# TensorE in the order of the source: grouped side work of the mixer and means of split operands in a two-layer decoder step

## Chip, cores and metric

The kernel runs on one core of a Trainium2 chip. The time is device time in microseconds (us) for one execution, which computes the whole decoder step. PE is TensorE (matmuls), DVE is VectorE, ACT is ScalarE, POOL is GpSimd, SP is SyncE, which only issues DMAs here.

## What is computed

A two-layer decoder trunk of width 1024 takes 256 prompt tokens and 8 sample sequences of 8 tokens. All 320 token columns go through the same weights in one pass.

```python
x += 1/2 * SwiGLU_1(RMSNorm(x))
h  = RMSNorm(x);  [u | v | q | g] = h @ W_in
A  = pool_mixer(u)            # trailing windows 2/4/8/16, a 256x256 map for each of 4 groups
B  = conv(v)                  # GLU, causal depthwise conv of width 31, LayerNorm, swish, W_pw
C  = cross_attend(q, k, v)    # 4 heads of 256 over 256 memory tokens
x += (sig(gA)*A + sig(gB)*B + sig(gC)*C) @ W_out
x += 1/2 * SwiGLU_2(RMSNorm(x))
```

For the prompt, memory keys and values come out of a projection of memory tokens; for the samples they are read from caches, and the pooling and the conv continue from stored rows. All numbers are float32.

## The kernel before

Activations lie feature-major: 8 tiles of 128 features by 320 tokens. Weights stream from HBM in the order of use; a unit is 8 blocks of 128x128. A product is exact to about float32 because weight and activation are each split in two fp32r halves (`whi`, `wlo`; `hhi`, `hlo`), and `chain` (L299) issues three matmuls for each block: hi*hi, hi*lo for the blocks of a unit, then lo*hi for them (L306, L307, L309). Eight blocks make a chain of 24 matmuls for one 128-feature output. `whi` is a cast on ACT, `wlo` a subtraction on DVE, or, for half of the units inside the mixer, a copy and an accumulating DMA on POOL's queue (L225 to L227). Splits run three units ahead of PE (`LA`).

Side work is a generator that `pump` (L276) steps once for each unit: the norm, the conv, pooling, softmax. `defer` (L257) puts a piece off by so many units. The program text thus gives every engine an order, but in the kernel before it is not the order that runs: the tile framework's scheduler, which simulates a timeline, may move instructions on every engine, PE too, as long as operands and buffers allow it. Engines then run their queues in order.

In the mixer of a layer (L683) PE projects memory keys and values, then v, q, and for each of four groups g two u chains, the two pool maps of the group before (short chains of two blocks), and two gate chains; then gates for branch C with the attention values, gates for branch B, W_pw and W_out. Small products lie between the chains:

- `prompt_scores` (L620 the scores of a head, L630 the four transposes of its softmax),
- `sample_scores` (L640: 8 matmuls for a batch, each 32 rows wide, in four column groups of the array), the transposes of its softmax (L652),
- the attention values of a block (L837) and of the samples (`sample_values`, L665), and the transposes of those (L677),
- means over features: a matmul with a constant matrix of 1/1024 in plain float32 (`mean_bc`, L354; the first one in eight pieces, L901). The prompt's norms, the memory and the conv's LayerNorm use them.

PSUM has eight banks: three under the tag `mm` for chains, two each under `cv` and `st`, one under `sa`. In a group the two u chains, two pool maps and two gate chains go through the three `mm` banks in turn, so the second pool map needs the bank of the first u chain, which ACT's copy to `ut` (L773) gives back, and the first gate chain needs that of the second u chain.

The depthwise conv of the prompt runs as two lanes of 31 multiply-adds on DVE in the `cv` banks (`conv_lane`), that of the samples on POOL (`conv_sample`), block after block; ACT moves each block's sample result to its place (L538), after DVE has ended the same block. Then the eight blocks are summed for the mean.

Of the kernel before, what the change touches and what calls it, by code (L numbers as in the profile page):

```python
# [7 lines left out]
F32 = mybir.dt.float32  # L8
# [7 lines left out]
P = 128  # L16
# [19 lines left out]
RC = 3.0  # L36
RN = 6.0
# [47 lines left out]
def trunk_kernel(  # L85
# [16 lines left out]
    nc = tc.nc  # L102
    const = ctx.enter_context(tc.tile_pool(name="const", bufs=1))
# [55 lines left out]
    ones = const.tile([P, P], F32, name="ones")  # L159
    pool.memset(ones[:, :], 1.0 / 1024.0)  # L160
# [191 lines left out]
    def mean_bc(acc, n, tag="st"):  # L352
# [21 lines left out]
    def ffn(h, mean, on_block, at_down=None):  # L374
# [8 lines left out]
        def stat():  # L383
            rsqrt_now(mean(), T, rstd[:, :])

        defer(stat, 2)
        for j in range(NJ):
            pg = pwide()
            chain(pg[:, :T], xs, T)
            sg = t320("sg")  # L390
# [6 lines left out]
            if j == 0:  # L397
                chain(pu[:, :T], xs, T)
                ev_gate()
            else:  # L400
                ev_gate()
                chain(pu[:, :T], xs, T)
            up = t320("up")
            dve.tensor_tensor(out=up[:, :], in0=pu[:, :T], in1=rstd[:, :], op=ALU.mult)
            dve.tensor_tensor(out=up[:, :], in0=up[:, :], in1=sg[:, :], op=ALU.mult)

            def fin(j=j, up=up):
                split_plain(up[:, :], *ref(j))

            defer(fin)  # L410
# [24 lines left out]
    def mem_operands(l, box):  # L435
# [20 lines left out]
        if l == 0:  # L456
            m = mean_bc(acc[:, :NM], NM)
            yield
            rsqrt_now(m, NM, rmem[:, :])
# [81 lines left out]
    def conv_gen(l, z, zdone, ch, gate):  # L541
# [32 lines left out]
        var = mean_bc(work[0], T, "cv")  # L574
# [96 lines left out]
    def sample_out(po, ats, g):  # L671
        ex = tp.tile([P, 2, NM], F32, name=nm("exo"), tag="ex", bufs=2)
        nc.scalar.copy(ex[:, 0, :], po[:, :256])
        yield
# [8 lines left out]
    def mixer(l, mh, acc, on_block):  # L683
        hn = []

        def norm_gen():
            rsqrt_now(mean_bc(acc[:, :], T), T, rstd[:, :])
# [13 lines left out]
        defer(lambda: start("norm", norm_gen(), 4), 2)  # L701
# [62 lines left out]

        for g in range(4):
# [3 lines left out]
            start("att", prompt_scores(q, g), 1)  # L769
# [57 lines left out]
        for o in range(KB):  # L827
            pc = pmm()
            chain(pc[:, :T], xs, T)
            s = t320("sgc")  # L830
            nc.scalar.activation(s[:, :TP], pc[:, :TP], AF.Sigmoid)
            nc.scalar.activation(sgs[:, o, :], pc[:, TP:T], AF.Sigmoid)
            hd, e = divmod(o, 2)
            pv = pst()
            clk["pe"] += 0.86
            for mb in range(2):
                nc.tensor.matmul(pv[:, :TP], vt[:, mb, o * P:o * P + P], kt[:, 2 * hd + mb, :],  # L837
                                 start=(mb == 0), stop=(mb == 1))

            def ev(o=o, s=s, pv=pv):  # L840
                dve.tensor_tensor(out=s[:, :TP], in0=pv[:, :TP], in1=s[:, :TP], op=ALU.mult)
                dve.tensor_tensor(out=merged[:, o, :TP], in0=merged[:, o, :TP], in1=s[:, :TP], op=ALU.add)

            defer(ev)
            if o == 0:
                drain("ss")
            if o == 1:
                pool_maps(3)
            if o % 4 == 0:
                drain("so")  # L850
                po = psum("sa", 1)
            if o % 2 == 1:
                sample_values(l, pps[o // 4], po, o - 1)
                sample_values(l, pps[o // 4], po, o)
# [41 lines left out]
    def first_mean():  # L896
        m = pst()
        for o in range(KB):
            s = t320("sq")
            pool.tensor_tensor(out=s[:, :], in0=x[:, o, :], in1=x[:, o, :], op=ALU.mult)  # L900
            nc.tensor.matmul(m[:, :T], ones[:, :], s[:, :], start=(o == 0), stop=(o == KB - 1))  # L901
# [160 lines left out]
```

## Time and profile before

| | us |
|---|---|
| median of 3 runs | 1659.54 |
| lowest, highest | 1659.35, 1659.97 |
| the profiled execution | 1659.87 |
| its span (mean granted TensorE clock 0.997) | 1657.9 |
| PE busy | 1630.5 (98%) |
| DVE busy | 1120.4 (68%) |
| ACT busy | 784.0 (47%) |
| POOL busy | 266.7 (16%) |

Matmuls overlap: one that streams 320 columns is shown with some 310 ns, while the next starts 147 ns after it. The spacing of starts is what counts, and busy shares say little about PE. A plain float32 matmul appears as two records. Lines in the trace are those of the kernel before.

### The profile page before, as it was taken

To read this page: it belongs to the slowest core of one execution; us is meant where nothing else is said; L and a number is where in the kernel's file an instruction comes from. 1 tells how busy PE (TensorE), PEld (TensorE's weight loads), DVE (VectorE), ACT (ScalarE), POOL (GpSimd) and SP (SyncE) were. 2 spreads that over 40 slices of the span, in tenths; PEclk is the share of its full clock that TensorE was granted. 3 is DMA by queue.
4 is the path that set the end of the run, shared out by engine and by line. 5 is a ranking of instruction groups with operands and counts; after the bars stand their busy time and mean duration, and the time that the engine had idled before them with its cause. 6 is when DMAs were issued, how large, how long until landed. Compare 5 with 4: busy or idle time off the path is not lost.

```text
span 1657.9 us, 27271 instructions
## 1 busy us (share of the span) xinstructions
PE 1630.5 (98%) x11194; PEld 1585.8 (96%) x11194; DVE 1120.4 (68%) x1854; ACT 784.0 (47%) x1167; POOL 266.7 (16%) x292
## 2 busy tenths in 40 slices
PE   8999999999999999999999999999999999999996
PEld 7999999998889999999999999999988899999996
DVE  7555647999975675554565564579998757655543
ACT  5444534456665444443344443354566544444341
POOL 2000001677520000000000000046674000000000
PEclk9999999999999999999999999999999999999998
DMA  7444446978976444444444444577798754444430
GB/s 276 153 151 145 169 169 199 266 231 238 294 260 229 151 155 151 144 146 149 149 153 153 153 153 166 189 220 232 235 278 254 267 199 153 145 145 147 150 126 32
DMA packets 47325, 305.73 MB, mean 184 GB/s; under 512 B 5728, under 2 KB 5792, under 8 KB 14048
## 3 DMA queue, kind: packets, MB, share of 16 engines
q1 hardware_dynamic: 38160, 270.75, 45.4%
q0 software_dynamic: 8752, 32.90, 9.2%
q8 instruction: 88, 1.44, 0.3%
q10 hardware_dynamic: 288, 0.33, 0.1%
q14 instruction: 37, 0.30, 0.0%
HBM read 295.14 MB, written 8.82 MB: 183 GB/s over the span
## 4 chain that ended last, share of the span: by engine, by line
PE 86%; DVE 7%; issue 3%; DMA 3%; ACT 1%; POOL 0%; DVEq 0%; SPq 0%; ACTq 0%; POOLq 0%
PE mm L306 19%; PE mm L309 19%; PE mm L307 19%; PE cv L309 8%; PE cv L306 8%; PE cv L307 8%; DVE cv L124 3%; DMA raw<-in_kc 2%; DVE us L124 1%; DVE wlo L124 1%; PE sa L665 1%; PE mm L484 1%; PE mm L483 1%; PE mm L487 1%; PE st L837 1%
## 5 line engine op out<-in xcount | busy, mean ns | idle before, releaser
L124 DVE TENSOR_TENSOR wlo<-raw,whi 128x1024 fp32r<-128x1024 f32 (+1 forms) x403 | 498.6, 1238 | 196.2 <-PE mm L309 85.7
L232 ACT CAST whi<-raw 128x1024 fp32r<-128x1024 f32 (+1 forms) x403 | 420.6, 1045 | 428.3 <-PE mm L307 252.9
L306 PE MATMUL mm<-hhi,whi 128*128 128x320 f32 x1712 | 512.3, 313 | 7.6 <-ACT hhi L358 5.8
L307 PE MATMUL mm<-hlo,whi 128*128 128x320 f32 x1712 | 507.8, 310 | 0.0
L306 PEld LDWEIGHTS mm<-hhi,whi 128*128 128x128 f32 x1712 | 321.6, 188 | 16.2 <-ACT hhi L358 6.6
L307 PEld LDWEIGHTS mm<-hlo,whi 128*128 128x128 f32 x1712 | 321.8, 188 | 1.9 <-DVE hlo L124 0.6
L309 PE MATMUL mm<-hhi,wlo 128*128 128x320 f32 x1712 | 289.4, 310 | 1.7 <-DMA wlo<-in_w 1.7
L309 PEld LDWEIGHTS mm<-hhi,wlo 128*128 128x128 f32 x1712 | 260.4, 188 | 2.7 <-DMA wlo<-in_w 2.2
L124 DVE SCALAR_TENSOR_TENSOR cv<-z,cst,cv 128x256 f32<-128x256 f32 x464 | 194.6, 476 | 0.2
L307 PE MATMUL cv<-hlo,whi 128*128 128x320 f32 x592 | 175.0, 310 | 0.0
L306 PE MATMUL cv<-hhi,whi 128*128 128x320 f32 x592 | 173.9, 309 | 0.0
L124 POOL MEMSET z<- 128x120 f32 x4 | 0.8, 196 | 820.5 <-PE mm L307 820.5
L124 POOL TENSOR_TENSOR pr<-pr 128x512 f32<-128x512 f32 (+3 forms) x128 | 122.7, 959 | 7.2
L306 PE MATMUL mm<-hidh,whi 128*128 128x320 f32 x418 | 123.9, 309 | 0.0
L307 PE MATMUL mm<-hidl,whi 128*128 128x320 f32 x418 | 123.7, 309 | 0.0
L362 ACT CAST hidh<-up 128x320 fp32r<-128x320 f32 x88 | 40.0, 459 | 159.8 <-DVE up L124 159.8
L307 PEld LDWEIGHTS cv<-hlo,whi 128*128 128x128 f32 x592 | 111.0, 188 | 0.2
L306 PEld LDWEIGHTS cv<-hhi,whi 128*128 128x128 f32 x592 | 110.8, 188 | 0.0
L309 PE MATMUL cv<-hhi,wlo 128*128 128x320 f32 x592 | 98.8, 309 | 0.0
L309 PEld LDWEIGHTS cv<-hhi,wlo 128*128 128x128 f32 x592 | 89.9, 188 | 0.2
L124 DVE TENSOR_TENSOR up<-mm,rstd 128x320 f32<-128x320 f32 x53 | 26.0, 490 | 87.8 <-PE mm L309 87.8
L306 PE MATMUL cv<-hidh,whi 128*128 128x320 f32 x286 | 84.7, 309 | 0.0
(196 smaller groups left out, 2336.2 us busy)
## 6 DMA issues: line engine op xcount, KB each, us to landing
raw<-in_w SPq DMA_DIRECT2D x221, 1024.0 KB, 4.8
wlo<-in_w POOLq DMA_DIRECT2D x42, 512.0 KB, 7.1
raw<-in_kc SPq DMA_DIRECT2D x16, 1024.0 KB, 7.3
raw<-in_vc SPq DMA_DIRECT2D x16, 1024.0 KB, 6.0
out_co<-z POOLq DMA_DIRECT2D x16, 135.0 KB, 6.4
raw<-in_mem SPq DMA_DIRECT2D x2, 1024.0 KB, 4.8
out_mk<-kt POOLq DMA_DIRECT2D x2, 1024.0 KB, 5.1
out_mv<-va POOLq DMA_DIRECT2D x2, 1024.0 KB, 9.5
```

Source lines behind the costliest of these rows:

```text
L124: return op(*args, **kw)
L232: nc.scalar.copy(h, r)
L306: nc.tensor.matmul(out, hi, xh, start=(i + e == 0), stop=False)
L307: nc.tensor.matmul(out, hi, xl, start=False, stop=False)
L309: nc.tensor.matmul(out, lo, xh, start=False, stop=(i + e == last))
L362: nc.scalar.copy(hi, src)
L483: nc.tensor.matmul(pv[mb][:, :], mh[0][:, k, mb * P:mb * P + P], wh, start=(k == 0), stop=False)
L484: nc.tensor.matmul(pv[mb][:, :], mh[1][:, k, mb * P:mb * P + P], wh, start=False, stop=False)
L487: nc.tensor.matmul(pv[mb][:, :], mh[0][:, k, mb * P:mb * P + P], wl, start=False, stop=(k == KB - 1))
L665: nc.tensor.matmul(po[32 * h:32 * h + 32, :256], pp[:, at:at + 32], raw[:, mb * 1024 + h * 256:mb * 1024 + h * 256 + 256], start=(bb == 0 ...
L837: nc.tensor.matmul(pv[:, :TP], vt[:, mb, o * P:o * P + P], kt[:, 2 * hd + mb, :], start=(mb == 0), stop=(mb == 1))
```

## The change

PE's instructions are no longer scheduled: `tc.manual_schedule` keeps them in the order in which the source issues them. The other engines are scheduled as before. The source now says what PE shall do between chains:

- The scores of a head come after both sample score batches of the group before (`attend`), its transposes some three chains later. A sample cache pair is 16 matmuls in one piece, the values of two blocks are taken together with both sample value batches (one `ev` for two blocks, over 512 columns).
- Means, apart from the first and the last, take an fp32r pair: `mean_split` casts on ACT and subtracts on DVE, `mean_bc` issues two fp32r matmuls. The split is made a unit or more ahead. In the conv, `2 * RL` = 8 steps lie between the split and the mean, and the side generator is stepped `RL` = 4 times for each unit from the sum on.
- The first mean's eight matmuls come as one piece after two chains. In an FFN the mean also comes after two chains, and the evictions of the first gate and up chains are held back until then.

```diff
+    ctx.enter_context(tc.manual_schedule(engines={mybir.EngineType.PE}))
...
+    def mean_split(acc, n):
+        hi, lo = (tp.tile([P, T], F32R, name=nm(i), tag="t320", bufs=7)[:, :n] for i in ("mh", "ml"))
+        split_plain(acc, hi, lo)
+        return hi, lo
+
+    def mean_bc(pair, n, tag="st"):
         m = psum(tag, 2)
-        nc.tensor.matmul(m[:, :n], ones[:, :], acc, start=True, stop=True)
+        nc.tensor.matmul(m[:, :n], onesr[:, :], pair[0], start=True, stop=False)
+        nc.tensor.matmul(m[:, :n], onesr[:, :], pair[1], start=False, stop=True)
         return m[:, :n]
...
-        yield
+        side["conv"][1] = RL
+        pair = mean_split(ysum[:, :], T)
+        for _ in range(2 * RL):
+            yield
...
-        mu = mean_bc(ysum[:, :], T, "cv")
+        mu = mean_bc(pair, T, "cv")
...
-        defer(lambda: start("norm", norm_gen(), 4), 2)
+        pair = []
+        defer(lambda: pair.append(mean_split(acc[:, :], T)))
+        defer(lambda: start("norm", norm_gen(), 4), 3)
...
+        def attend(h):
+            gen = prompt_scores(q, h)
+            next(gen)
+            start("att", gen, 1)
+
+        attend(0)
         for g in range(4):
...
-            start("att", prompt_scores(q, g), 1)
...
+            drain("ss")
+            drain("att")
             sample_scores(l, qz, sc, 2 * g)
             sample_scores(l, qz, sc, 2 * g + 1)
-            drain("att")
+            if g < 3:
+                attend(g + 1)
...
+            pv = pst()
+            clk["pe"] += 1.72
+            for i in range(2):
+                for mb in range(2):
+                    c = o - 1 + i
+                    nc.tensor.matmul(pv[:, i * TP:i * TP + TP], vt[:, mb, c * P:c * P + P], kt[:, o - 1 + mb, :],
+                                     start=(mb == 0), stop=(mb == 1))
...
     def first_mean():
+        def part():
+            m = pst()
+            for o in range(KB):
+                s = t320("sq")
+                pool.tensor_tensor(out=s[:, :], in0=x[:, o, :], in1=x[:, o, :], op=ALU.mult)
+                nc.tensor.matmul(m[:, :T], ones, s[:, :], start=(o == 0), stop=(o == KB - 1))
+            return m[:, :T]
+        return part
```

Where the rows below come from the changed kernel, its lines are: chain L309, L310, L312 (before L306, L307, L309), scores L644, transposes L654, sample scores L664, copy of u L805, sample conv result L556, split for a mean L371.

PE at the start of the projection of v in layer 0, right after the norm of the mixer; before, from the middle of it (`cv_2735`, `cv_2766` and `mm_2798` are three chains' banks):

```order
L306 MATMUL cv_2735<-hhi_2483,whi_2636 128x320
L307 MATMUL cv_2766<-hlo_2484,whi_2667 128x320
L307 MATMUL cv_2735<-hlo_2484,whi_2636 128x320
L306 MATMUL cv_2735<-hhi_2483,whi_2636 128x320
L306 MATMUL cv_2766<-hhi_2483,whi_2667 128x320
L307 MATMUL cv_2766<-hlo_2484,whi_2667 128x320
L306 MATMUL cv_2766<-hhi_2483,whi_2667 128x320
L307 MATMUL mm_2798<-hlo_2484,whi_2699 128x320
L306 MATMUL mm_2798<-hhi_2483,whi_2699 128x320
```

and in the changed kernel, the end of the first chain and the begin of the second:

```order
L309 MATMUL cv_2747<-hhi_2527,whi_2640 128x320
L310 MATMUL cv_2747<-hlo_2528,whi_2640 128x320
L309 MATMUL cv_2747<-hhi_2527,whi_2640 128x320
L310 MATMUL cv_2747<-hlo_2528,whi_2640 128x320
L312 MATMUL cv_2747<-hhi_2527,wlo_2641 128x320 x8
L309 MATMUL cv_2778<-hhi_2527,whi_2678 128x320
L310 MATMUL cv_2778<-hlo_2528,whi_2678 128x320
```

Three and more chains were interleaved while the last pieces of `hlo` were made; now a chain follows the other, so the first needs all of `hhi` and `hlo` at once.

PE in group 1 of layer 0, between the pool maps and the first gate chain before (`raw_4113` and `raw_4123` are the caches of two sample batches):

```order
L309 MATMUL mm_4250<-plh_4027,wlo_4064 128x320 x2
L640 MATMUL sa_4005<-raw_4113,qz_3572 32x256 x2
L630 MATMUL st_4337<-cst,ex_4189 128x128
L640 MATMUL sa_4005<-raw_4113,qz_3572 32x256 x2
L630 MATMUL st_4337<-cst,ex_4189 128x128 x3
L640 MATMUL sa_4005<-raw_4113,qz_3572 32x256 x4
L640 MATMUL sa_4005<-raw_4123,qz_3572 32x256
L306 MATMUL mm_4258<-hhi_2483,whi_4063 128x320
```

and the same caches in the changed kernel, after the second gate chain:

```order
L310 MATMUL mm_4326<-hlo_2528,whi_4197 128x320
L312 MATMUL mm_4326<-hhi_2527,wlo_4198 128x320 x4
L664 MATMUL sa_4020<-raw_4131,qz_3584 32x256 x8
L664 MATMUL sa_4020<-raw_4141,qz_3584 32x256 x8
L644 MATMUL st_4395<-kt,qa_3583 128x256 x4
L309 MATMUL mm_4404<-hhi_2527,whi_4197 128x320
```

The second cache's other seven matmuls stood elsewhere before; now both caches are one run of 16, with the next head's scores behind them, and the transposes are in a run of their own.

ACT in group 3 of layer 0, before (`ut_4629` gets the two u chains, `ex_4687` is the softmax of head 3, `pr_4237` the sample conv of block 6):

```order
L602 ACT_TABLE_LOAD
L602 ACTIVATE ex_4687,sm_4689<-st_4647,mx_4688 128x256 x2
L773 COPY ut_4629<-mm_4632 128x320
L538 ACTIVATE z_2730<-pr_4237,cst 128x64
L225 CAST whi_4721<-raw_4555 128x1024
L607 ACTIVATE ex_4687<-ex_4687,sm_4689 128x256 x2
L773 COPY ut_4629<-mm_4677 128x320
L226 ACTIVATE wlo_4722<-raw_4555 128x1024
```

and in the changed kernel (`ut_4646`, `ex_4664`, and `pr_4526`, the sample conv of block 7):

```order
L626 ACT_TABLE_LOAD
L626 ACTIVATE ex_4664,sm_4666<-st_4641,mx_4665 128x256 x2
L235 CAST whi_4697<-raw_4471 128x1024
L631 ACTIVATE ex_4664<-ex_4664,sm_4666 128x256 x2
L805 COPY ut_4646<-mm_4649 128x320
L556 ACTIVATE z_2742<-pr_4526,cst 128x64
L371 CAST mh_4832<-ysum_2819 128x320
L228 CAST whi_4736<-raw_4567 128x1024
L805 COPY ut_4646<-mm_4696 128x320
L229 ACTIVATE wlo_4737<-raw_4567 128x1024
L235 CAST whi_4772<-raw_4567 128x1024
```

The sample conv result of the last block and the cast of the conv's sum (`mh_4832`) now stand ahead of the second copy of u; before, the former came 14 places later, and there was no such cast.

## Rows read from the trace of the kernel before

**Rows 1.** The page, part 1: busy us of each engine (share of the span).

```profile
PE 1630.5 (98%) x11194; PEld 1585.8 (96%) x11194; DVE 1120.4 (68%) x1854; ACT 784.0 (47%) x1167; POOL 266.7 (16%) x292
```

**Rows 2.** The page, part 5: line engine op, out<-in xcount | busy us, mean ns of one | idle before.

```profile
L232 ACT CAST whi<-raw 128x1024 fp32r<-128x1024 f32 (+1 forms) x403 | 420.6, 1045 | 428.3 <-PE mm L307 252.9
...
L124 DVE SCALAR_TENSOR_TENSOR cv<-z,cst,cv 128x256 f32<-128x256 f32 x464 | 194.6, 476 | 0.2
...
L362 ACT CAST hidh<-up 128x320 fp32r<-128x320 f32 x88 | 40.0, 459 | 159.8 <-DVE up L124 159.8
```

**Rows 3.** Waits of PE: engine line waited for: total us, times, longest.

```profile
PE sa L640 <- DMA raw<-in_kc: 2.8, 3, 1.7
PE mm L309 <- DMA wlo<-in_w: 2.3, 3, 1.4
PE mm L306 <- ACT ut L773: 2.1, 3, 1.0
```

**Rows 4.** Timeline of PE, a whole run of sample values (start, us, line, tile, count).

```profile
473.28 0.46 PE L309 MATMUL mm<-plh,wlo 128*128 128x320 f32 x2
473.67 1.93 PE L665 MATMUL sa<-raw,qz 128*32 128x256 f32 x32
...
475.93 0.31 PE L306 MATMUL mm<-hhi,whi 128*128 128x320 f32 x1
```

**Rows 5.** Timeline of PE, broken sample scores of layer 0, then the next chain.

```profile
405.82 0.46 PE L309 MATMUL mm<-plh,wlo 128*128 128x320 f32 x2
406.20 0.63 PE L640 MATMUL sa<-raw,qz 128*32 128x256 f32 x4
...
409.43 0.31 PE L306 MATMUL mm<-hhi,whi 128*128 128x320 f32 x1
```

**Rows 6.** Timeline of PE, layer 0: head scores, two values, transposes.

```profile
376.38 1.89 PE L620 MATMUL st<-kt,qa 128*128 128x256 f32 x8
...
464.70 1.02 PE L837 MATMUL st<-kt,va 128*128 128x256 f32 x4
...
512.37 0.38 PE L677 MATMUL st<-cst,exo 128*128 128x128 f32 x2
```

**Rows 7.** Timeline of PE: last piece of the first mean; the third chain.

```profile
15.91 0.70 PE L901 MATMUL st<-sq,ones 128*128 128x320 f32 x2
...
16.60 0.31 PE L307 MATMUL mm<-hlo,whi 128*128 128x320 f32 x1
...
19.97 0.31 PE L306 MATMUL mm<-hhi,whi 128*128 128x320 f32 x1
```

**Rows 8.** Timeline of PE and DVE where the first projection after the norm starts.

```profile
269.47 0.46 PE L306 MATMUL cv<-hhi,whi 128*128 128x320 f32 x2
...
273.42 0.49 DVE L124 TENSOR_TENSOR hlo<-hf,hhi 128x320 fp32r<-128x320 f32 x1
```

**Rows 9.** Timeline of PE and DVE where w_out starts after w_pw.

```profile
565.38 0.31 PE L306 MATMUL mm<-mgh,whi 128*128 128x320 f32 x1
...
568.13 0.49 DVE L124 TENSOR_TENSOR mgl<-merged,mgh 128x320 fp32r<-128x320 f32 x1 [0.53 <-ACT mgh L362]
```

**Rows 10.** Timeline of PE: the gate chain of group 3 starts, layers 0 and 1.

```profile
452.76 0.39 PE L306 MATMUL mm<-hhi,whi 128*128 128x320 f32 x1
...
1269.43 0.39 PE L306 MATMUL mm<-hhi,whi 128*128 128x320 f32 x1
```

**Rows 11.** Timeline of DVE: one split, and the last head's scaled maximum.

```profile
408.11 1.36 DVE L124 TENSOR_TENSOR wlo<-raw,whi 128x1024 fp32r<-128x1024 f32 x1
...
444.36 0.15 DVE L124 TENSOR_SCALAR mx<-mx 128x2 f32<-128x2 f32 x1
```

**Rows 12.** Timeline of ACT, layer 0: sample conv results of blocks 5 and 7.

```profile
411.40 0.35 ACT L538 ACTIVATE z<-pr,cst 128x64 f32<-128x64 f32 x1 [2.65 <-POOL pr L124]
...
467.73 0.34 ACT L538 ACTIVATE z<-pr,cst 128x64 f32<-128x64 f32 x1
```

**Rows 13.** Timeline of POOL: the sample conv of block 5 starts.

```profile
397.69 2.00 POOL L124 TENSOR_TENSOR pr<-z,cst 128x1024 f32<-128x1024 f32 x1 [1.64 <-ACT z L538]
```

More of the change, by code (lines that the diff above doesn't have):

```diff
@@ L158, in trunk_kernel @@
     nc.scalar.dma_start(cst[:, :8], c_in[:, :8])
-    ones = const.tile([P, P], F32, name="ones")
-    pool.memset(ones[:, :], 1.0 / 1024.0)
+    onesr = const.tile([P, P], F32R, name="ones")
+    ones = onesr[:, :].bitcast(F32)
+    pool.memset(ones, 1.0 / 1024.0)
     ident = cst[:, C_ID:C_ID + P]
@@ L389, in ffn @@
             chain(pg[:, :T], xs, T)
+            if j == 1:
+                for fn in held:
+                    fn()
             sg = t320("sg")
@@ L396, in ffn, with ev_up @@
             pu = pwide()
-            if j == 0:
-                chain(pu[:, :T], xs, T)
+            if j:
                 ev_gate()
             else:
-                ev_gate()
-                chain(pu[:, :T], xs, T)
+                held.append(ev_gate)
+            chain(pu[:, :T], xs, T)
             up = t320("up")
[L404 to L410, printed above, removed]
+            def ev_up(pu=pu, up=up, sg=sg, j=j):
+                dve.tensor_tensor(out=up[:, :], in0=pu[:, :T], in1=rstd[:, :], op=ALU.mult)
+                dve.tensor_tensor(out=up[:, :], in0=up[:, :], in1=sg[:, :], op=ALU.mult)
+                defer(lambda: split_plain(up[:, :], *ref(j)))
+            if j:
+                ev_up()
+            else:
+                held.append(ev_up)
         flush()
@@ L456, in mem_operands @@
         if l == 0:
-            m = mean_bc(acc[:, :NM], NM)
+            pair = mean_split(acc[:, :NM], NM)
             yield
-            rsqrt_now(m, NM, rmem[:, :])
+            yield
+            rsqrt_now(mean_bc(pair, NM), NM, rmem[:, :])
+            for _ in range(4):
+                yield
             m2 = pst()
@@ L573, in conv_gen @@
             yield
-        var = mean_bc(work[0], T, "cv")
+        pair = mean_split(work[0], T)
+        for _ in range(2 * RL):
+            yield
+        var = mean_bc(pair, T, "cv")
         r = tp.tile([P, T], F32, name=nm("lnr"), tag="ysum", bufs=1)
@@ L673, in sample_out @@
         nc.scalar.copy(ex[:, 0, :], po[:, :256])
-        yield
+        for _ in range(8):
+            yield
         tr = pst()
@@ L896, in first_mean, with later_mean, split @@
     def first_mean():
[L897 to L901, printed above, removed]
-        return m[:, :T]
+        def part():
[6 more added lines that the diff above has]
+        return part
+    def later_mean(st):
+        def split():
+            pair = mean_split(st.acc[:, :], T)
+            return lambda: mean_bc(pair, T)
+        return split
     mean = first_mean
@@ L947, in trunk_kernel @@
     m = pst()
-    nc.tensor.matmul(m[:, :T], ones[:, :], fst.acc[:, :], start=True, stop=False)
-    nc.tensor.matmul(m[:, :T], ones[:, :], last[:, :], start=False, stop=True)
+    nc.tensor.matmul(m[:, :T], ones, fst.acc[:, :], start=True, stop=False)
+    nc.tensor.matmul(m[:, :T], ones, last[:, :], start=False, stop=True)
     rsqrt_now(m[:, :T], T, rstd[:, :])
```

52 lines of the change are left out of this document (26 added, 26 removed).

## Prediction

> **What bounds the kernel now.** I began with the page's busy times: PE is busy for 98% of the span [rows 1], so the time is PE's instruction stream plus its waits. The list of PE's waits comes next. Apart from the wait for the first operands at the start there is little in it: 2.8 us for cache transfers, 2.3 us for `wlo` transfers, 2.1 us for ACT's copies of u [rows 3]. So a gain must come from a shorter stream on PE, and a loss from new waits.
>
> What a stream is worth is read from the spacing of starts. From the second matmul of a chain to the first of the next are 23 steps, 16.60 to 19.97 us: 0.147 us each [rows 7]. A run of side work between chains is then priced by how much later a matmul of the next chain starts than at that spacing. Sixteen sample matmuls in one piece: the last chain matmul before them starts at 473.43, the third one after would be due at 473.87, and starts at 475.93: 2.06 us [rows 4]. The broken run of group 1 is 9 sample matmuls with the four transposes of a head among them. The same way, it is due at 406.41, starts at 409.43, and costs 3.02 us [rows 5]. In one piece, 9/16 of 2.06 and two pairs of transposes at 0.22, priced by the same rule, [rows 6] would be 1.60. The matmuls of four column groups run together, and a four that is cut costs as much as a whole one. This is what the grouping can save.
>
> **The sum, step by step.** The profiled execution took 1659.87 us, 0.33 over the median of the runs shown. I work on it and subtract that.
>
> *Grouping in the mixer.* Between the first run of layer 0 (376.38) and the last (512.37) [rows 6] there are 23 runs. Priced as above they come to 40.2 us, and 42.3 in layer 1, waits inside them counted. The same work in whole pieces: four head scores at 1.72, eight pairs of head transposes and four other pairs at 0.22, four sample score and four sample value pieces at 2.06, eight values at 0.86 [rows 4, 6], and two means of two fp32r matmuls each, 4 x 0.147. That is 33.5 us a layer. The stream gets shorter by 6.7 and 8.8: 15.5 us.
>
> *Means.* A plain float32 mean costs 0.54 (the chain matmul after it starts 0.69 behind it instead of 0.15) [rows 7]; two fp32r matmuls cost 0.29. There are five such outside the conv and a smaller one for the memory: -1.4. Their new casts and subtractions are on ACT and DVE, a unit ahead, where both have room outside the mixer; without that room each would put some 0.9 us in front of a norm.
>
> *First mean.* Its eight matmuls lay in waits for the first operands, all but the last one; now they stand in one piece in front of the third chain, which began at 19.97 [rows 7]. 8 x 0.54, less the 0.54 of the piece that delayed it before: +3.7.
>
> *Norm.* PE reaches the projection of v at 269.47. The last `hlo` ends on DVE at 273.91 [rows 8]. Interleaving covered this. In order, the matmul that needs it is the 16th, due 15 x 0.147 later, at 271.67, and DVE's queue has one more `hlo` (0.4) ahead of it: a wait of 2.7, in each layer: +5.4. Everything on PE is behind it.
>
> *W_out.* The same at the step from W_pw: chain at 565.38, its 16th matmul due at 567.58, `mgl` done at 568.62 [rows 9]: 1.05 for each layer, +2.1.
>
> *wlo transfers.* The waits for them [rows 3] come from buffers that the interleaved chains held. Two of the three lie right behind the norm, and 1.7 of the 2.3 us go: -1.7. At worst they stay.
>
> *Who can keep up in the mixer.* This decides. Take the point where PE, through with the u chains and pool maps of group 3, starts its first gate chain: 452.76 in the kernel before [rows 10]. From 376.38 up to there the runs cost 21.0 us in layer 0, and whole pieces of what the new order has there 14.6. So without new waits the chain starts 6.4 earlier, at 446.4, and behind it the two streams are equal within 0.4: nearly all of this layer's gain must be made before that point. The gate chain needs the bank that ACT's second copy of u frees. In ACT's new order, that copy stands behind three things: the exponentials of head 3, the sample conv result of the last block, and the cast of the conv's sum, with a `whi` cast between.
>
> - Exponentials: DVE went from the split at 408.11 to the scaled maximum at 444.36 in 36.3 us [rows 11], without a pause. In its new order seven conv steps less lie between these, at 0.42 [rows 2]: 441.4. With the exponentials, a `whi` and the scaling behind it, ACT gets to the first copy near 445.
> - Sample conv: POOL started block 5 at 397.69 [rows 13] and ACT had to wait 2.65 for it until 411.40 [rows 12], so a block takes 13.7. The last block can start when ACT has taken the result of block 6, which follows the last conv step of that block on DVE. In the new order that is 18 us of DVE's work behind the split at 408.11, with ACT's copy near 430. Block 7 is then ready at 444 at best; before, its result was taken at 467.73 [rows 12].
> - The sum of the conv (0.45), its cast (0.46), a `whi` (1.05) [rows 2] and the copy itself (0.4) follow one after the other: 2.4 us. The gate chain can start at 447 at the earliest.
>
> Between 447 and 452.76, the time at which it starts now, I take 449.5, nearer to the early end: the 444 is a best case, and POOL's queue has some 2 us of DMA issues and small operations between whose place I cannot read. That gives back 3.1 of the gain in each layer: 6.2. Bounds: nothing (the copies are in time), and 6.4 in each layer.
>
> The sum: -15.5 + 6.2 - 1.4 + 3.7 + 5.4 + 2.1 - 1.7 = -1.2. From 1659.87 to 1658.7, and less the 0.33: **1658.3 us**. DMAs: SyncE issues the same transfers in the same order; sample caches are asked for later than before, so the 2.8 us of waits for them [rows 3] are counted as gone with the runs, and a POOL queue that is late costs through the conv above.
>
> **The rivals.**
>
> *A, faster: the mixer keeps up.* If DVE, which no longer waits for chains that end late, runs ahead, the copies are in time and the 6.2 us stay: 1652.1. For it: the new order of DVE already has the conv seven steps further at the same split. Against it: DVE had no pause there in 36 us, and two slow engines must both be early. If half of the norm's waits also go, 1649.4.
>
> *B, slower: the sample conv holds ACT.* If the last block's result comes at 450 or later, the second copy comes at 452.4 or later, the gate chain starts no earlier than at present, and the side work's gain before that point is gone: 12.8 instead of 6.2 us given back, 1664.9. It decides from 449.5 on: the gate chain is then at 451.9, 5.5 are given back in each layer, and the time passes 1662.9. For it: before, ACT waited for this very engine with nothing else done meanwhile [rows 12]; the whole queue behind stood. [...] Against it: POOL would need some 20 us from 430 instead of 13.7 to be that late.
>
> *C, nothing moves.* If fp32r means cost as much as before, and the broken runs cost what they do because of the kinds of matmul that alternate, not because of cut fours, the grouping saves only what the number of runs falls by: 16 of 23 remain, a third of 15.5, 5.2 us, with no copy late since PE is then no earlier. Nothing comes from the means: 5.4 + 2.1 + 3.7 - 1.7 - 5.2 = +4.3, or 1663.8. What speaks against it is in [rows 4, 5].
>
> **How the numbers follow.** A measurement of this kernel can tell about 0.2%, 3.3 us, from no change: "same" is 1656.2 to 1662.9. The forecast, 2 to 5.5 us given back in each layer, holds 0.42, nearly all of it "same". A has 0.32, all faster. B has 0.18, and C with waits I did not see 0.08, all slower. Faster 0.32, same 0.42, slower 0.26. The likeliest case alone is 1656 to 1663; the range runs from A to B, 1651 to 1667, which leaves out about 2 in 10: A with the norm's waits halved, and several losses together.
>
> **What would show it.** In the changed profile: whole pieces of 16 sample matmuls at 2.06 and no transposes among them; eight pieces of the first mean in front of the third chain; a wait of PE for `hlo` of 2 to 3 us in each layer and about 1 for `mgl`; waits for `wlo` mostly gone; and PE's wait for ACT's copy `ut`, some 3 us in all before the gate chain of group 3, behind the sample conv's result on ACT. No such wait means A; one of 6 or more means B. I would be wrong in kind if PE waited somewhere that this text does not name.

## The result, and the profile after

The changed kernel takes **1696.57 us** (1695.08 to 1697.12), against 1659.68 for the kernel before on the same chip: a ratio of 1.0221, interval [1.0203, 1.0239]. It is 37 us slower. The forecast was 1658.3, the range ended at 1667. The profiled execution took 1695.08, its span 1693.0.

The page, part 1, of the changed kernel; it answers to [rows 1]:

```profile
PE 1641.3 (97%) x11194; PEld 1597.0 (94%) x11194; DVE 1142.2 (67%) x1848; ACT 794.0 (47%) x1181; POOL 274.9 (16%) x292
```

PE has as many matmuls as before and its busy share falls by one point. DVE does six instructions less and is busy 21.8 us longer; POOL does the same and is busy 8.2 us longer. Part 5 says which instructions of DVE:

```profile
L126 DVE TENSOR_TENSOR wlo<-raw,whi 128x1024 fp32r<-128x1024 f32 (+1 forms) x403 | 511.4, 1270 | 189.6 <-PE mm L312 81.6
L235 ACT CAST whi<-raw 128x1024 fp32r<-128x1024 f32 (+1 forms) x403 | 420.7, 1046 | 422.5 <-PE mm L310 249.8
...
L126 DVE SCALAR_TENSOR_TENSOR cv<-z,cst,cv 128x256 f32<-128x256 f32 x464 | 195.5, 478 | 0.8
```

Casts on ACT (1045 ns [rows 2], now 1046) and the conv steps on DVE (476, now 478) last as long as before. The subtraction `wlo`, with two operands in SBUF, does not: 1270 ns in the mean, 1238 before.

Where the time went is read from the start of the same chain in both traces. Chains are counted in blocks of 24 matmuls; each row says how much longer a stretch lasts than in the kernel before. The last two columns are experiments 1 and 11 below.

| stretch (chain blocks) | in the sum | after | scheduled PE | no conv on POOL |
|---|---|---|---|---|
| start to the third chain (0-2) | +3.7 | +4.7 | -0.3 | +3.9 |
| to the first scores (2-102), with the norm and the projections of v and q | +2.7 | +3.4 | +1.0 | +4.6 |
| mixer of layer 0 (102-131) | -6.7 +3.1 | **+12.1** | -2.3 | -6.9 |
| w_out, FFNs (131-285) | +1.05 | +1.3 | -0.4 | +1.3 |
| the same stretch of layer 1 (285-320) | +2.7 | +2.1 | 0.0 | +3.4 |
| mixer of layer 1 (320-349) | -8.8 +3.1 | **+10.4** | -4.1 | -8.6 |
| to the end | +1.05 | +1.3 | -0.2 | +1.3 |
| all | -1.2 | +35.15 | -6.2 | -1.0 |

The column of the sum leaves the means (-1.4) and the transfers of `wlo` (-1.7) to its last row, as they lie in several stretches.

So 22.5 us are lost in two stretches where 9.3 were to be gained. PE's waits in the changed kernel, to be held against [rows 3]:

```profile
PE mm L309 <- ACT ut L805: 22.9, 8, 5.6
...
PE cv L310 <- DVE hlo L126: 2.7, 4, 1.0
...
PE mm L312 <- DMA wlo<-in_w: 0.4, 1, 0.4
```

The waits for caches are gone and those for `wlo` nearly so (0.4), as forecast, and `ut` has grown from 2.1 to 22.9 us. The timeline of PE in the changed kernel (start, us, line, tile, count, idle before and its releaser):

```profile
20.61 4.47 PE L942 MATMUL st<-sq,ones 128*128 128x320 f32 x16
24.67 0.55 PE L309 MATMUL mm<-hhi,whi 128*128 128x320 f32 x1
...
275.85 0.42 PE L310 MATMUL cv<-hlo,whi 128*128 128x320 f32 x1 [0.40 <-DVE hlo L126]
277.61 0.41 PE L309 MATMUL cv<-hhi,whi 128*128 128x320 f32 x1 [0.54 <-ACT hhi L720]
278.99 0.41 PE L310 MATMUL cv<-hlo,whi 128*128 128x320 f32 x1 [0.97 <-DVE hlo L126]
...
418.99 0.64 PE L309 MATMUL mm<-plh,whi 128*128 128x320 f32 x1 [4.97 <-ACT ut L805]
...
422.00 0.63 PE L309 MATMUL mm<-hhi,whi 128*128 128x320 f32 x1 [1.04 <-ACT ut L805]
422.43 0.47 PE L310 MATMUL mm<-hlo,whi 128*128 128x320 f32 x1
422.69 0.47 PE L309 MATMUL mm<-hhi,whi 128*128 128x320 f32 x1
...
491.75 0.45 PE L312 MATMUL mm<-plh,wlo 128*128 128x320 f32 x2
492.05 0.38 PE L676 MATMUL st<-cst,exs 128*128 128x128 f32 x2
492.26 1.89 PE L881 MATMUL st<-kt,va 128*128 128x256 f32 x8
494.08 1.93 PE L689 MATMUL sa<-raw,qz 128*32 128x256 f32 x32
...
496.35 0.31 PE L309 MATMUL mm<-hhi,whi 128*128 128x320 f32 x1
...
588.35 0.41 PE L309 MATMUL mm<-mgh,whi 128*128 128x320 f32 x1 [0.56 <-ACT mgh L371]
```

Three readings. First, the whole pieces cost what the prediction said: the next matmul of a chain would have been due at 492.05 and the third one 0.29 later, at 492.34; it started at 496.35, 4.01 us late. Two values, 16 sample matmuls and a pair of transposes were priced 2 x 0.86 + 2.06 + 0.22 = 4.00 [rows 4, 6]. Second, PE stands 4.97 us ahead of the second pool map of group 1 of layer 0; the same happens in group 3 (4.24) and in both groups of layer 1 (5.64, 5.23). Third, after such a wait matmuls start 0.267 apart instead of 0.147 (422.43, 422.69). The windows of that stretch (us; busy time and count of PE, PEld, DVE, ACT, POOL; granted clock; DMA share; GB/s):

```profile
411.00:414.00 3.00, 2.63 (x17) 2.12 (x15) 3.00 (x6) 0.00 (x0) 2.26 (x4) 1.00 1.01 345
414.00:417.00 3.00, 0.01 (x1) 0.00 (x0) 2.61 (x8) 1.86 (x4) 0.00 (x0) 1.00 0.92 385
417.00:420.00 3.00, 1.01 (x4) 1.01 (x5) 2.53 (x8) 3.00 (x7) 1.30 (x1) 0.58 0.04 16
420.00:423.00 3.00, 1.96 (x8) 1.56 (x8) 3.00 (x7) 1.94 (x4) 3.00 (x4) 0.50 0.10 11
423.00:426.00 3.00, 3.00 (x14) 2.96 (x14) 3.00 (x3) 1.45 (x2) 2.84 (x5) 0.50 1.05 202
426.00:430.00 4.00, 4.00 (x24) 4.00 (x24) 4.00 (x5) 2.85 (x4) 3.47 (x5) 0.78 1.03 334
```

PE does nothing between 414 and 417, and is then granted 0.50 until 427.7, though it has work again from 418.99. ACT does nothing from 411 to 414, while DVE is busy throughout. What ACT waits for, in its list of waits:

```profile
ACT L626 <- DVE mx L126: 42.6, 8, 7.9
...
ACT z L556 <- POOL pr L126: 3.8, 4, 1.8
```

and in the kernel before:

```profile
ACT L602 <- DVE mx L124: 12.0, 2, 6.0
...
ACT ex L602 <- DVE mx L124: 3.5, 4, 1.4
```

The list has an entry of 42.6 us for the softmax's maximum (`mx`), 12.0 + 3.5 before; the sample conv result (`z`), on which the prediction put its weight, takes 3.8. ACT's timeline shows what stands behind the maximum:

```profile
415.13 1.28 ACT L626 ACT_TABLE_LOAD   x1 [7.93 <-DVE mx L126]
...
418.27 0.35 ACT L556 ACTIVATE z<-pr,cst 128x64 f32<-128x64 f32 x1
418.52 0.42 ACT L805 COPY ut<-mm 128x320 f32<-128x320 f32 x1
```

The copy that frees PE's bank lasts 0.42 us; ACT stands 7.93 us at the maximum, and the copy comes behind the exponentials, a `whi` cast and a sample conv result, though PE had ended its chain by 408.98. DVE's timeline in that stretch, conv steps mostly left out (`us` is a sum over pooling windows, `pll` the low half of the split pooled input):

```profile
398.52 2.25 DVE L126 TENSOR_TENSOR wlo<-raw,whi 128x1024 fp32r<-128x1024 f32 x1
...
401.08 2.39 DVE L126 TENSOR_TENSOR us<-ut 128x540 f32<-128x540 f32 x2
...
407.19 2.93 DVE L126 TENSOR_TENSOR wlo<-raw,whi 128x1024 fp32r<-128x1024 f32 x1
...
410.44 1.53 DVE L126 TENSOR_TENSOR pll<-us,plh 128x640 fp32r<-128x640 f32 x1
...
413.46 0.68 DVE L126 TENSOR_REDUCE mx<-st 128x2 f32<-128x512 f32 x1
...
414.89 0.15 DVE L126 TENSOR_SCALAR mx<-mx 128x2 f32<-128x2 f32 x1
```

and POOL's beside its second half, the sample conv:

```profile
407.19 1.85 POOL L126 TENSOR_TENSOR pr<-z,cst 128x960 f32<-128x960 f32 x1
409.11 4.38 POOL L126 TENSOR_TENSOR pr<-pr 128x512 f32<-128x512 f32 x4
```

The `wlo` at 407.19 starts with POOL's product of that time and ends at 410.12, 1.1 us after the product; `pll` at 410.44 lies beside POOL's sums. By themselves they last 1.22 and 0.81 (run 14, below). In the kernel before, the same operations stand ahead of the same maximum (there at 400.75), but at their short times; POOL's product begins only at 397.69 [rows 13]:

```profile
391.16 1.15 DVE L124 TENSOR_TENSOR us<-ut 128x540 f32<-128x540 f32 x2
...
395.56 1.21 DVE L124 TENSOR_TENSOR wlo<-raw,whi 128x1024 fp32r<-128x1024 f32 x1
...
397.08 0.81 DVE L124 TENSOR_TENSOR pll<-us,plh 128x640 fp32r<-128x640 f32 x1
```

So the new order did not put these operations ahead of the maximum; it made them fall beside POOL's conv.

### The profile page after: what moved, and what is told of

The parts are those of the page before. It is cut to its first block, busy times and chain, and to the rows that moved or that the text cites. A ratio compares the mean times of both kernels' runs of the same rounds, so it can differ in the third digit from the quotient of the medians.

```text
span 1693.0 us, 27271 instructions
## 1 busy us (share of the span) xinstructions
PE 1641.3 (97%) x11194; PEld 1597.0 (94%) x11194; DVE 1142.2 (67%) x1848; ACT 794.0 (47%) x1181; POOL 274.9 (16%) x292
## 5 line engine op out<-in xcount | busy, mean ns | idle before, releaser
L126 DVE TENSOR_TENSOR wlo<-raw,whi 128x1024 fp32r<-128x1024 f32 (+1 forms) x403 | 511.4, 1270 | 189.6 <-PE mm L312 81.6
L235 ACT CAST whi<-raw 128x1024 fp32r<-128x1024 f32 (+1 forms) x403 | 420.7, 1046 | 422.5 <-PE mm L310 249.8
L309 PE MATMUL mm<-hhi,whi 128*128 128x320 f32 x1712 | 516.2, 315 | 9.4 <-ACT hhi L367 6.4
L310 PE MATMUL mm<-hlo,whi 128*128 128x320 f32 x1712 | 512.3, 313 | 0.3 <-DVE hlo L126 0.2
L309 PEld LDWEIGHTS mm<-hhi,whi 128*128 128x128 f32 x1712 | 326.0, 190 | 16.4 <-ACT hhi L367 6.8
L310 PEld LDWEIGHTS mm<-hlo,whi 128*128 128x128 f32 x1712 | 325.7, 190 | 3.8 <-DVE hlo L126 3.5
L312 PE MATMUL mm<-hhi,wlo 128*128 128x320 f32 x1712 | 291.2, 311 | 0.0
L312 PEld LDWEIGHTS mm<-hhi,wlo 128*128 128x128 f32 x1712 | 263.4, 190 | 0.0
L310 PE MATMUL cv<-hlo,whi 128*128 128x320 f32 x592 | 175.8, 311 | 2.7 <-DVE hlo L126 2.7
L309 PE MATMUL cv<-hhi,whi 128*128 128x320 f32 x592 | 175.1, 309 | 1.1 <-ACT hhi L720 1.1
L126 POOL TENSOR_TENSOR pr<-pr 128x512 f32<-128x512 f32 (+3 forms) x128 | 131.1, 1024 | 7.1
L310 PE MATMUL mm<-hidl,whi 128*128 128x320 f32 x418 | 123.7, 309 | 0.0
L309 PE MATMUL mm<-hidh,whi 128*128 128x320 f32 x418 | 123.7, 309 | 0.0
L371 ACT CAST hidh<-up 128x320 fp32r<-128x320 f32 x88 | 40.3, 459 | 165.7 <-DVE up L126 165.7
L310 PEld LDWEIGHTS cv<-hlo,whi 128*128 128x128 f32 x592 | 111.1, 188 | 4.4 <-DVE hlo L126 4.0
L309 PEld LDWEIGHTS cv<-hhi,whi 128*128 128x128 f32 x592 | 111.1, 188 | 1.5 <-ACT hhi L720 1.5
L312 PE MATMUL cv<-hhi,wlo 128*128 128x320 f32 x592 | 98.8, 309 | 0.0
L312 PEld LDWEIGHTS cv<-hhi,wlo 128*128 128x128 f32 x592 | 89.8, 188 | 0.0
L309 PE MATMUL cv<-hidh,whi 128*128 128x320 f32 x286 | 84.7, 309 | 0.0
```

The costliest lines, as they stand in the source:

```text
L126: return op(*args, **kw)
L235: nc.scalar.copy(h, r)
L309: nc.tensor.matmul(out, hi, xh, start=(i + e == 0), stop=False)
L310: nc.tensor.matmul(out, hi, xl, start=False, stop=False)
L312: nc.tensor.matmul(out, lo, xh, start=False, stop=(i + e == last))
L371: nc.scalar.copy(hi, src)
```

## Experiments

The theory with which I began: in a fixed order PE meets banks that ACT's late copies hold, and the scheduler had filled those places with other work. The rivals: the price lies in the grouping, in the maximum itself, in the clock, or in what POOL does. Each edit moves more than it names, since the scheduler orders ACT, DVE and POOL anew. Ratios are to the kernel before, run beside them; differences in us are to 1659.68 and 1696.57 above.

**1 and 2. The order alone.** The changed kernel with PE scheduled again, and the kernel before with PE in source order.

```diff
 1: changed kernel
-    ctx.enter_context(tc.manual_schedule(engines={mybir.EngineType.PE}))
 2: kernel before
+    ctx.enter_context(tc.manual_schedule(engines={mybir.EngineType.PE}))
```

> The change without its line on the manual order: PE is scheduled again, the source's grouping, deferrals and split means stay. Theory 1 (the fixed order lets PE stand at banks that ACT frees late, 23 us, and the clock falls behind these waits, some 15 us): PE's waits for the copies of u fall below 4 us and the time comes to 1650 to 1662. Theory 2 (the new source itself costs: first mean in one piece, means later, evictions held back, exponentials ahead of copies): the time stays above 1680, with the waits where they are.

> The kernel before with PE in the order of its source, nothing else. Theory 1: PE stands at late operands as in the change: waits of PE above 15 us in all beside the start, time 1680 to 1705. Theory 2 (the order alone does little, the regrouped source makes the loss): 1655 to 1670.

Measured: 1654.1, 0.9962 [0.9947, 0.9977], and 1701.11, 1.0247 [1.0232, 1.0262]. The order alone costs 42.5 us on the new source and 41.4 on the old one; all else in the change is worth 5.6 us in its favour where PE is scheduled, 4.5 where it is not. With the order of the source the old kernel loses 24.8 us in the two mixer stretches, the new one 22.5: the grouping neither caused nor softened that. PE's waits in the first of the two runs begin with

```profile
PE mm L308 <- ACT hhi L366: 5.7, 1, 5.7
PE mm L311 <- DMA wlo<-in_w: 2.8, 3, 1.5
```

No `ut` is among them. Its timeline shows the broken runs of the kernel before again (two sample matmuls, a transpose, two, three transposes, five, between the pool maps and the gate chain of group 1). Two sample matmuls take 0.56 us there (406.00 to 406.56), four of a whole run 0.47 (a quarter of 494.08 to 495.95 in the changed kernel): these are the cut fours that the prediction counted. But this run lasts from 406.00 to 408.83, and ACT's second copy of u, whose bank the gate chain needs, ends at 407.38 there: about half of the run stands in what would have been a wait.

**3. Is it the maximum?** The softmaxes take no maximum.

```diff
-        dve.reduce_max(mx[:, :n], sc, axis=AX.X)
...
-            nc.scalar.activation(e[:, i, :], sc[:, i, :], AF.Exp, bias=mx[:, i:i + 1], scale=0.0625,
+            nc.scalar.activation(e[:, i, :], sc[:, i, :], AF.Exp, scale=0.0625,
```

> The change without the subtraction of the row maximum in the softmaxes of the attention (left out: the maximum and the bias it gives; the exponentials no longer wait for DVE). Theory 1a (ACT stands at the exponentials until DVE, busy with the conv, has made the maximum, and the copies of u stand behind): PE's wait for the copies falls from 22.9 us to under 8, and with it the clock's loss: 1660 to 1675. Rival 1b (the copies are held by the sample conv of POOL, or by the transfers of whi): the wait stays above 15 us, 1688 or more.

Measured: 1677.54, 1.0103 [1.0086, 1.012]. PE's waits for `ut` fall from 22.9 to 0.9, so the maximum is what ACT's queue stands at. But 19 of 37 us come back, not all: waits for `wlo` transfers (6.7) and for DVE's `merged` (5.7) take their place. DVE is late for `merged` (the gated sum of the branches) too, not only for the maximum.

**4. The clock.** 36 unused matmuls ahead of the second pool map of groups 1 and 3.

```diff
+                if i == 1 and g in (0, 2):
+                    warm = pst()
+                    for n in range(36):
+                        nc.tensor.matmul(warm[:, :T], onesr[:, :], xs[n % 8][0], start=True, stop=True)
```

> The change with 36 matmuls that compute nothing used (5.3 us) in front of the second pool map of groups 1 and 3, where PE waits for the bank. Theory 3 (the granted clock halves behind these waits and that costs some 15 us beside them): granted clock above 0.995, wait for the copies below 6 us, 1680 to 1686. Rival (the clock's fall costs nothing, since ACT and DVE set the pace there): 1695 or more.

Measured: 1705.74, 1.0271 [1.0256, 1.0286], a miss. The unused matmuls are some 21 us in all, about what the four waits lasted (20.1). The granted clock stays at 1.00 in group 1, and the transposes after its first gate chain come at 424.16 instead of 425.36. But the scheduler gave the other engines another order, and waits of 5.00 and 4.92 appear in group 2 of the two layers, where there were none; the clock falls to 0.50 there (the mean of the run is 0.990, 0.987 in the changed kernel). The clock's price is not settled by this run.

**5 and 6. Cover by hand.** ACT in source order too, with the exponentials two steps later; and one sample score pair between the two pool maps.

```diff
 5
+    ctx.enter_context(tc.manual_schedule(engines={mybir.EngineType.PE, mybir.EngineType.Activation}))
...
+        for _ in range(2):
+            yield
 6: between() is both sample score batches of the group, in groups 1 to 3
...
+                if i == 1 and between is not None:
+                    between()
...
```

> The change with the exponentials of a head put two steps later in the source and ACT in the order of its source too, so that both copies of u stand ahead of the exponentials in groups 1 and 3; all of the work is the same. Theory 1a (the copies are late only because they stand behind exponentials that wait for DVE): PE's wait for the copies falls from 22.9 us to below 6; some of it may come back as waits for the transposes' input; time 1665 to 1682. Rival 1c (DVE and POOL set the pace of the mixer, the copies only show it): other waits take the place, time 1688 or more.

> The change with the whole piece of 16 sample score matmuls of a group moved between the two pool maps of the group, where PE stands (groups 1 to 3); in the kernel before, parts of this work lay there. Theory 1d (the small products between the chains were the cover of that wait, and grouping them elsewhere laid it bare): the waits for the copies of u fall by 2.06 us for each group that waits, from 22.9 to 14 to 18, and the time by 6 to 12, to 1684 to 1691. Rival 1c (the pace is set by DVE and POOL, so PE's order inside a group is of no matter): 1694 or more.

Measured: 1702.92, 1.0256 [1.0239, 1.0272], and 1690.62, 1.0182 [1.0167, 1.0197]. In the first, no wait for `ut` is left, and PE waits for the exponentials instead (15.3), for a `whi` (7.6) and for gates (7.2). In the second, `ut` falls to 7.0, and waits for the sample softmax (4.5), caches (3.6) and `wlo` (4.6) come. A piece in one place covers one wait.

**7 and 8. Two small terms.** Means of split operands in the kernel before; and the first mean of the changed kernel as one pair, its squares summed on POOL.

```diff
 7: kernel before, in mean_bc
-        nc.tensor.matmul(m[:, :n], ones[:, :], acc, start=True, stop=True)
+        split_plain(acc, hi, lo)
+        nc.tensor.matmul(m[:, :n], onesr[:, :], hi, start=True, stop=False)
+        nc.tensor.matmul(m[:, :n], onesr[:, :], lo, start=False, stop=True)
...
 8: changed kernel, in first_mean
...
+            pool.tensor_tensor(out=a[:, :], in0=a[:, :], in1=s[:, :], op=ALU.add)
```

> The kernel before, scheduled, with only its means (all but the first and last) as two fp32r matmuls on a split operand. The change without the manual order was 5.5 us faster than the kernel before. Theory 4a (the means are a small part): 1657 to 1659.5. Theory 4b (they are most of it): 1653 to 1656.

> The change with the first mean taken from squares that POOL adds up first, as one pair of fp32r matmuls at the same place, instead of eight plain ones. If the eight in one piece cost PE 4.3 us that nothing covers: 1691 to 1693.5, and the third chain starts some 4 us earlier. If later evictions eat it: 1695 or more.

Measured: 1657.79, 0.9986 [0.9977, 0.9996], 1.9 us less in the two traces, near the 1.4 of the sum, though the interval spans 0.7 to 3.8; and 1699.87, 1.0241 [1.0226, 1.0256], a miss: the third chain starts 6.3 us later than before instead of 4.7, since PE waits 4.8 for the sum's cast.

**9 and 10. Is DVE short of time because of the conv?** 16 instead of 31 multiply-adds, in the changed kernel and in the one before.

```diff
-            for k in range(1, TAPS):
+            for k in range(1, 16):
```

> The change with 16 of the 31 taps of the prompt's depthwise conv on DVE (15 left out, some 50 us of DVE in each mixer). Theory 5 (in the first half of the mixer DVE has no time to spare, so its late maxima hold ACT and PE; with room on DVE the fixed order costs only the first mean, the norm and w_out): waits for the copies of u below 4 us, 1650 to 1662, within 6 us of the kernel before with the same taps. Rival (a fixed order of PE is slow with any DVE): 1680 or more.

> The kernel before with 16 of the 31 taps of the prompt's conv, as the measure for the run beside it. Theory 5 (PE is the bound with DVE just keeping pace): 1650 to 1658, a few us gained where PE waited for ACT. Rival (DVE is the bound of this kernel's mixer): below 1645.

Measured: 1691.48, 1.0188 [1.0173, 1.0204], and 1668.4, 1.005 [1.0035, 1.0065]. In the changed kernel DVE loses 100 us of work (1041.4 busy), and PE's waits begin with

```profile
PE cv L362 <- ACT mh L371: 12.9, 2, 7.0
PE mm L312 <- DMA wlo<-in_w: 7.9, 3, 4.9
...
PE mm L309 <- ACT ut L805: 1.9, 2, 1.0
```

Half of the theory holds: the waits for `ut` are nearly gone, 1.9 instead of 22.9, and the two mixer stretches lose 3.2 and 2.4 instead of 12.1 and 10.4. So how much DVE has to do ahead of the maximum does matter. The time was still missed, with a gain of 5 us: PE now waits 12.9 for the cast of the conv's sum, whose mean comes at 419.21 instead of 488.24 in layer 0, and 7.9 for transfers of `wlo`. The kernel before becomes slower too, by 7.0 and 4.8 us ahead of the first scores of the two layers, while its mixers are 0.5 and 2.2 shorter; why is not shown.

**11 and 12. Without the sample conv on POOL**, in both kernels.

```diff
-                pool.tensor_tensor(out=pr[:, 0:n, :], in0=win, in1=wv, op=ALU.mult)
+                if half == 0:
+                    pool.tensor_copy(pr[:, 0, :], win[:, 0, :])
...
-                    pool.tensor_tensor(out=pr[:, 0:m, :], in0=pr[:, 0:m, :], in1=pr[:, m:2 * m, :], op=ALU.add)
```

> The change without the sample conv's products and sums on POOL (left out; one small copy for each block stays). Theory 6 (DVE's operations with two SBUF operands stand while a POOL operation runs, 6 us more in each layer than before, and ACT stands at late results of POOL): splits on DVE at 1.2 us, DVE busy 15 us or more below 1142, and 1668 to 1684. Rival (the loss comes from the order of DVE's queue alone): 1688 or more.

> The kernel before without the sample conv's products and sums on POOL, as the measure for the run beside it. Theory 6: DVE busy falls by 5 to 10 us, the time by 0 to 5: 1654 to 1659.5, since its PE has other work where DVE is late. [...]

Measured: 1658.7, 0.999 [0.998, 1.0], and 1655.69, 0.9977 [0.9968, 0.9987]. POOL's conv costs the changed kernel 38 us and the one before 4 to 5. DVE is busy 1093.5 us instead of 1142.2 in the changed kernel, with the same instructions. The page of the first run, and its wait for `ut`:

```profile
PE 1629.3 (98%) x11194; PEld 1588.3 (96%) x11194; DVE 1093.5 (66%) x1848; ACT 794.0 (48%) x1181; POOL 90.8 (5%) x132
```

```profile
PE mm L309 <- ACT ut L799: 0.7, 2, 0.3
```

**13 to 15. Is POOL late, or in the way?** In 13 the sample conv's result is moved by POOL, so that ACT never waits for it; in 14 every product and sum on POOL is replaced by two memsets, which keep POOL occupied but read nothing (one small copy for each block stays); 15 is 13 with PE scheduled.

```diff
 13 and 15
-            nc.scalar.activation(y[j][:, TP:T], pr[:, 0, :], AF.Identity, bias=ccol(l, C_BD, j))
+            pool.tensor_scalar(out=y[j][:, TP:T], in0=pr[:, 0, :], scalar1=ccol(l, C_BD, j), scalar2=None, op0=ALU.add)
 14
-                pool.tensor_tensor(out=pr[:, 0:n, :], in0=win, in1=wv, op=ALU.mult)
+                for _ in range(2):
+                    pool.memset(pr[:, 0:n, :], 0.0)
...
-                    pool.tensor_tensor(out=pr[:, 0:m, :], in0=pr[:, 0:m, :], in1=pr[:, m:2 * m, :], op=ALU.add)
+                    for _ in range(2):
+                        pool.memset(pr[:, 0:m, :], 0.0)
```

> The change with the bias and move of each sample conv result on POOL instead of ACT, so that ACT never stands at POOL's sums. Theory 6b (ACT, held by POOL's sums, is late with everything behind): the waits for the copies of u fall below 12 us and the time to 1684 or less. Theory 6a (POOL's operations stop DVE's two-operand ones, and ACT only stands at DVE's late maxima): splits and pooling sums on DVE as long as in the change, waits and time as there, 1690 or more.

> The change with every product and sum of the sample conv on POOL replaced by two memsets of the same size (left out: the sample conv's values), so POOL is still busy and ACT still takes its results in the same places, but POOL reads nothing. Theory 6a: DVE's splits in the mixer come to 1.2 us, its busy time below 1115, waits for the copies of u under 5 us, 1655 to 1672. Theory 6b (POOL's duration is what counts): with POOL busy in the mixers within 20% of the change, the waits stay and the time is 1685 or more.

> The change without the manual order (1654.1 us) and with the sample conv results moved by POOL: a candidate. If ACT's stands at POOL cost PE anything there, 1650 to 1653; if the other work covers them, 1653 to 1656.

Measured: 13, 1687.41, 1.0161 [1.0145, 1.0176], with 18.3 us of `ut` waits left; 14, 1661.59, 1.0003 [0.9994, 1.0012], with 2.7 left; 15, 1657.86, 0.9982 [0.9973, 0.9991], a miss, and no better than experiment 1 (0.9962). Run 14 decides. Its page, and ACT's wait for the sample conv:

```profile
PE 1629.6 (98%) x11194; PEld 1588.6 (96%) x11194; DVE 1092.8 (66%) x1848; ACT 793.9 (48%) x1181; POOL 228.4 (14%) x468
```

```profile
ACT z L560 <- POOL pr L126: 12.4, 4, 5.9
```

POOL's conv, its busy time over the 90.8 of run 11, still takes 138 us of 184, and ACT waits three times as long for its results as in the changed kernel (12.4 against 3.8). Yet DVE is as fast as without any conv on POOL (1092.8), and 35 us of the loss are gone. So what hurts is not that POOL is late, but what its products and sums do beside DVE; unlike the memsets they read, and no run takes that apart from the rest. The same stretch of DVE as above, with the same instructions in the same order, in run 14:

```profile
396.28 1.23 DVE L126 TENSOR_TENSOR wlo<-raw,whi 128x1024 fp32r<-128x1024 f32 x1
...
397.81 1.15 DVE L126 TENSOR_TENSOR us<-ut 128x540 f32<-128x540 f32 x2
...
402.61 1.22 DVE L126 TENSOR_TENSOR wlo<-raw,whi 128x1024 fp32r<-128x1024 f32 x1
...
404.13 0.81 DVE L126 TENSOR_TENSOR pll<-us,plh 128x640 fp32r<-128x640 f32 x1
...
407.87 0.15 DVE L126 TENSOR_SCALAR mx<-mx 128x2 f32<-128x2 f32 x1
```

From the start of that first `wlo` to the end of the scaled maximum are 11.7 us here and 16.5 in the changed kernel. These four groups make 4.7 of the difference of 4.8: 1.0 and 1.7 for the two `wlo`, 1.2 for `us`, 0.7 for `pll`. DVE had also come to the stretch later against PE: from the first scores of this head on PE to the maximum are 10.0 us in the changed kernel and 2.9 in run 14 (6.1 before, 2.5 in run 11, 3.2 in run 9). `us` and `pll` lie beside memsets all the time in run 14 (POOL's from 397.61 to 400.13 and from 403.50 to 408.65) and take 1.15 and 0.81, against 2.39 and 1.53 in the changed kernel. A `wlo` takes 1.22 us in run 14 against up to 2.93 beside products; run 14 had no stretched `wlo` (1.23 at most between 390 and 500).

## Why the prediction was wrong

The mechanism of the loss, by the runs: the order fixes PE to the second pool map right behind the u chains. The first copy of u stands behind the exponentials on ACT, these behind the maximum on DVE, and that behind operations of two SBUF operands, which last longer beside POOL's conv (a `wlo` up to 2.93 us, against 1.22 in run 14). PE idles 4 to 6 us at four places, and the granted clock falls to 0.50 after each. Taking away either half nearly removes it: the order (1654.1) or POOL's products and sums (1661.59 with memsets in their place). It is DVE's lateness that counts, not POOL alone: with a shorter conv on DVE, run 9, the waits for `ut` went as well (1.9 us left), though not the time.

- **Failed: "Who can keep up in the mixer"**, the term "given back 6.2". The two stretches lost 22.5 instead of gaining 9.3: 31.8 of the 36.4 us between the sum and the trace (35.15 + 1.2). Three things in it were wrong. It looked at one place, the gate chain of group 3; the waits begin in group 1, and at the first copy of u. It took DVE's times from the old order as fixed and counted only conv steps (0.42 each; they start 0.39 apart there, a matter of 0.2 us); in the new order `us`, `wlo` and `pll`, which stood ahead of the maximum before as well, fall beside POOL's conv and last longer (4.7 us more than in run 14 in the stretch read above). In group 3 the scaled maximum was done at 464.4, where 441.4 was forecast; PE was 15.7 us behind by then, and the other 7.3 are DVE's. And its upper bound, 6.4 in each layer, was no bound: it supposed that the worst case is PE where it was before. A wait in a fixed order is not limited by the gain that led to it.
- **The clock was not in the sum.** Changed kernel and experiment 11 differ by 36.2 us in their spans. Waits for `ut` are 22.2 of it, for exponentials and `wlo` 1.5, the first mean 0.8; 11.6 remain. They are not simply the clock's price, since run 11 is not free of it: it is granted 0.50 from 278.7 to 282.1 and from 1091.0 to 1094.5 (its mean is 0.995, 0.997 in the kernel before), behind the two norms, where the changed kernel keeps 1.00, and its stretches with the norms are 1.3 longer each. In the mixers alone 14.2 remain. An estimate from the trace: behind its four waits the changed kernel works 25.3 us at 0.50, with starts 0.267 instead of 0.147 apart, which makes 11.4. Experiment 4, meant to show the price, did not.
- **Grouping: -15.5 was right in size, in part by luck.** Without POOL's conv both stretches last 134.84 us, 6.9 and 8.6 less than before. But in the kernel before, the conv's removal alone shortens them by 2.3 and 2.8: with POOL's conv out of both, the arrangement gains 4.5 and 5.8, 10.3 in all. So up to a third of the 15.5 may have been waits that POOL caused, which I had counted as cost of the arrangement.
- **The broken runs were cover.** The prediction priced them as loss. Scheduled PE put them where a bank was not yet free, for about half of the run read above; experiment 1 has them again and is the fastest. How much of its gain is cover is not shown.
- **First mean, +3.7: measured +4.7.** The piece lasts from 20.61 to 24.67, or 4.06. **Norm, 2.7 each:** waits of 0.40, 0.54 and 0.97, 1.9 in layer 0. With all else there, transfers included, the stretches around both norms are 3.4 and 2.1 longer, 5.5 against 3.7 in the sum (5.4 less the 1.7 for transfers). **W_out, 1.05 each:** 0.56 of wait, stretches 1.3 longer. **`wlo`, -1.7:** waits fall from 2.3 to 0.4. **Means, -1.4:** -1.9 by themselves. Together the terms outside the mixers came out 4.6 us worse than in the sum.
- **Rivals.** A fell. B has the right sign and a wrong holder: ACT stood 42.6 us at the maximum and 3.8 at the sample conv, and run 13, which frees ACT of the latter, still waits 18.3. Its 1664.9 had the same false limit. C fell with the price of whole pieces (its 5.2, for 7 runs of 23, should have been 4.7).

Even with POOL out of the way (experiment 11) the change gains 15.5 in the mixers and gives back 14.5 elsewhere: 3.9 at the first mean, 8.1 in the stretches with the norms, 2.5 at W_out. It draws level with the kernel before, and stays 4.6 us behind the scheduled one, which still has POOL's conv.

Open: the exact share of the clock, what in POOL's products and sums holds DVE up, why 13 still gains 9 us, and why a shorter conv on DVE (9 and 10) makes transfers of `wlo` late.

## What to carry to other kernels

When an engine gets a fixed order, list every place at which it takes a buffer back from another engine, and follow that engine's queue to what it stands behind, and from there to the next engine; the loss there is bounded by how late that can be, not by the gain. Pieces of work that look badly cut may be standing in a wait: price a run together with what would be idle without it. On DVE, put operations of two SBUF operands beside products and sums on POOL only where nothing waits for them: here a `wlo` took up to 2.93 us there instead of 1.22.

## What the runs showed of the hardware

- A `wlo` subtraction (128x1024, two SBUF operands) took 1.22 us in run 14, with memsets on POOL, and up to 2.93 beside its products. Conv steps, which accumulate in PSUM, did not change (476 ns before, 478 after, 481 in run 14).
- Over the whole kernel POOL's conv cost DVE 49 us of busy time (1142.2 against 1093.5 without it), in the kernel before 33 (1120.4 against 1087.4).
- After the wait of 4.97 us PE was granted 0.50 up to 427.7, though it had work again from 418.99; its matmuls of 320 columns then start 0.267 apart.
